# Routing logits placed by hand inside the next tile's output projection, and the normalised rows stored from ScalarE's queue

## The chip, the cores and the metric

The kernel runs on one core of a Trainium2 chip. The metric is device time in microseconds (us) of one execution. Engines are named as in the profile: PE is TensorE, DVE VectorE, ACT ScalarE, POOL GpSimd, SP SyncE; a "queue" is the list of DMAs that one of them issues.

## The reference

Two layers over 512 latent tokens of width 1024, in float32. Each layer adds a token mixer and then a mixture of experts to the stream, each behind an RMSNorm with shift and scale and in front of a gate:

```
for i in range(2):
    h  = modulate(x, norm_mix[i], shift, scale)
    y  = deltanet_mixer(h, ...) if i == 0 else shortconv_mixer(h, ...)    # both end in  ... @ w_out
    x  = x + gate_m * y
    hf = modulate(x, norm_ffn[i], shift_f, scale_f)
    pg = softmax(hf @ router_g[i]);  gi = argmax(pg)                      # one of 4 groups
    le = (hf @ router_e[i])[8 experts of that group];  top 2 of softmax(le)
    x  = x + gate_f * sum over the 2 experts of  weight * (silu(hf @ w1[e]) * (hf @ w3[e])) @ w2[e]
return rmsnorm(x, final_norm)
```

There are 32 experts per layer with a hidden width of 512. What the change touches lies between `x + gate_m * y` and the top 2: the last projection `@ w_out`, the gated sum, the norm, and the 36 logits (4 groups and 32 experts) of each token.

## The kernel before, in words

Tokens are held in four tiles of 128 in the on-chip stream `xs` (128 partitions, 4 tiles, 1024). Projections are computed as 128 by 512 blocks in PSUM: a job is one tile `t` and one half `n` of the 1024 output columns. Numbers are split into a high and a low part, so that a job takes 24 matmuls of 128 x 512: for each of 8 slices `k`, high by high, low by high, high by low.

Weights come as units of 2 MB through rings of buffers, nine units in all. SP issues these loads (`issue`, L214); a load whose buffer is still read waits, and what SP issues behind it waits too. Instructions are put into their order within each engine by a scheduler that models the time; a part of the program inside `manual_schedule` keeps the order in which it is written. Before, that holds for the expert stages only.

**Layer 0, end of the mixer** (`finish`). Eight jobs, first half 0 for all tiles, then half 1. A tile is made ready by `prepare` and `turn` (L1231 transposes, L1233 product on VectorE, L1234 high part on ScalarE, low part on GpSimd; the tiles are named `S`, `yhi`, `ylo`, and `vn`, `Ap` for tile 3). The matmuls are L1258 to L1260, into PSUM banks `pp` and `pj`; VectorE multiplies by the gate and adds the old stream (L1269, L1270). From job 5 on, `logits` of the tile finished one job earlier is written behind each job, and that of tile 3 at the end; the scheduler decides where its parts go.

**Logits of a tile** (`logits`). The norm (L340 to L342); eight transposes of `xs` into two PSUM banks (L351); a copy of each to SBUF, one on VectorE (L357), one on ScalarE (L355); eight matmuls of 128 x 36 with the router weights (L360), which the trace shows as two instructions each; the scaled sum into `L` (L361); the normalised row tile `xn` on ScalarE (L362), and its store to the DRAM scratch `hscr`, issued by SP (L363). The SBUF buffers for this are tiles that the mixer no longer needs (`z`, `kp`, `vp`, `xt`, `qe` in layer 0; `xn`, `whi`, `wlo` in layer 1).

**Routing** (`routing`). It waits for the logits of all tiles, then it is a long chain on VectorE (L1311 on) with a few matmuls (L1380); `ra` and `rb` (L1376, L1378) are written into memory that the logits' tiles have left. At its start SP issues three more weight units and the row of gates (L1286). At its end GpSimd gathers the token rows of the first experts from `hscr` (L1418), TensorE transposes them (L1428), and the expert stage begins (products L1442, L1469; transposes of the gate product L1457).

**Layer 1, end of the mixer** (`mixer1`). The first half of the output projection runs slice by slice for all four tiles into four banks (L1820 to L1822), then the second half tile by tile (L1834 to L1836). `add_out` is the gated sum of one job, a multiply (L1850) and an add (L1851) on VectorE; it is written for both halves of a tile behind the tile's second half, and the logits of the tile before behind that. Then the same routing follows.

The stretch from 548 us to the first experts of layer 0, and that from 1318 us to those of layer 1, are called tails below.

Of the kernel before, what the change touches and what calls it, by code (L numbers as in the profile page):

```python
# [13 lines left out]
AF = mybir.ActivationFunctionType  # L14
OP = mybir.AluOpType
# [4 lines left out]
D = 1024  # L20
# [3 lines left out]
EPS = 1e-6  # L24
# [9 lines left out]
class Net:  # L34
# [310 lines left out]
    def logits(self, l, t, xn, h, banks, lb):  # L345

        nc = self.nc
        r = self.norm(t, xn)
        ps = [self.bank(b) for b in banks]
        for c in range(8):  # L350
            nc.tensor.transpose(ps[c // 4][:, 128 * (c % 4):128 * (c % 4) + 128], self.xs[:, t, 128 * c:128 * c + 128], self.ident)  # L351
        for g in range(2):
            p = ps[g].rearrange("p (k d) -> p k d", k=4)
            if g:
                nc.scalar.activation(h[:, 4 * g:4 * g + 4], p, AF.Copy)  # L355
            else:
                nc.vector.tensor_copy(h[:, 4 * g:4 * g + 4], p)  # L357
        p = self.bank(lb)[:, :36]
        for c in range(8):
            nc.tensor.matmul(p, h[:, c], self.wr[:, l, c], start=(c == 0), stop=(c == 7))  # L360
        nc.vector.scalar_tensor_tensor(self.L[:, t], p, r, self.br[:, l], op0=OP.mult, op1=OP.add)  # L361
        nc.scalar.activation(xn, self.xs[:, t], AF.Copy, scale=r)  # L362
        nc.sync.dma_start(self.hscr[128 * t:128 * t + 128], xn)  # L363
# [823 lines left out]
    def finish(self, fp, wo):  # L1187

        nc, I, pb = self.nc, self.I, self.pb
        gt = fp.tile([128, 1024], F32, name="gt0", bufs=1)  # L1190
# [58 lines left out]
        def logits(t):  # L1249
            z, xt = ld[t]  # L1250
            self.logits(0, t, xt, z, ("pc", "ada"), "pc")
        for i, (t, n) in enumerate(jobs):
            yhi, ylo = ys[t]
            hi, lo = wo[n]
            ps = self.bank(("pp", "pj")[i % 2])
            for k in range(8):
                a, b = yhi[k // 4][:, k % 4], ylo[k // 4][:, k % 4]
                nc.tensor.matmul(ps, a, hi[:, k], start=(k == 0), stop=False)  # L1258
                nc.tensor.matmul(ps, b, hi[:, k], start=False, stop=False)
                nc.tensor.matmul(ps, a, lo[:, k], start=False, stop=(k == 7))  # L1260
            if i == 3:
                self.issue(self.taken - 1, 2)
            for u in ahead.get(i, ()):
                if u != 2:
                    prepare(u)
                ys[u] = turn(u)
            xt = ld[t][1]
            x = self.xs[:, t, 512 * n:512 * n + 512]
            nc.vector.tensor_tensor(x, ps, gt[:, 512 * n:512 * n + 512], op=OP.mult)  # L1269
            nc.vector.tensor_tensor(x, x, xt[:, 512 * n:512 * n + 512], op=OP.add)  # L1270
            if i > 4:
                logits(jobs[i - 1][0])
            if i == 7:
                logits(3)
                self.issue(self.taken, 1)
# [3 lines left out]
    def routing(self, l):  # L1279

        tc, nc, I, rt = self.tc, self.nc, self.I, self.rt
        with ExitStack() as cs:
# [3 lines left out]
            nc.sync.dma_start(self.gate, self.row(l, 2, 1))  # L1286
# [114 lines left out]
            nc.vector.tensor_copy(self.most, most)  # L1401

# [320 lines left out]
    def mixer1(self):  # L1723
        tc, nc, I, cp = self.tc, self.nc, self.I, self.cp
        with ExitStack() as cs:
# [3 lines left out]
            with ExitStack() as ws:  # L1729
# [95 lines left out]
                def logits(t):  # L1825
                    xn, h = (wk.tile([128, 8, 128], F32R, name=n).bitcast(F32) if t > 1 or n == "wlo" else
                             wk.tile([128, 8, 128], F32, name="xn") for n in ("whi", "wlo"))
                    self.logits(1, t, xn.rearrange("p k d -> p (k d)"), h, *(('tr', 'tr'), 'tr'))
                hi, lo = second
                for t in range(4):  # L1830
                    o = slice(128 * t, 128 * t + 128)
# [43 lines left out]
```

## Time and profile before

| | |
|---|---|
| three runs | 1878.93, 1885.66, 1885.20 us; median 1885.2 |
| the profiled execution | 1881.79 us, of which the span of instructions is 1880.0 us |
| granted clock of TensorE, mean over the span | 0.961 of full speed |
| TensorE busy | 1717.0 us, 91% of the span |
| VectorE, ScalarE, GpSimd busy | 43%, 26%, 22% |
| DMA | 307 GB/s of HBM traffic over the span; 425 GB/s in the expert stages |

The busy shares are averages over stages of different kinds. The timelines give the start of an instruction, or of several alike in a row, its duration, and in brackets how long its engine stood idle before it and what ended that. Matmuls overlap: each of 128 x 512 is shown with 0.39 us, and one starts every 0.23 us.

### The profile page before, as it was taken

To read this page: it belongs to the slowest core of one execution; us is meant where nothing else is said; L and a number is where in the kernel's file an instruction comes from. 1 tells how busy PE (TensorE), PEld (TensorE's weight loads), DVE (VectorE), ACT (ScalarE), POOL (GpSimd) and SP (SyncE) were. 2 spreads that over 40 slices of the span, in tenths; PEclk is the share of its full clock that TensorE was granted. 3 is DMA by queue.
4 is the path that set the end of the run, shared out by engine and by line. 5 is a ranking of instruction groups with operands and counts; after the bars stand their busy time and mean duration, and the time that the engine had idled before them with its cause. 6 is when DMAs were issued, how large, how long until landed. Compare 5 with 4: busy or idle time off the path is not lost. (4 is left out here: it accounts for less than half of the span.)

```text
span 1880.0 us, 26579 instructions
## 1 busy us (share of the span) xinstructions
PE 1717.0 (91%) x10245; PEld 988.9 (53%) x10246; DVE 812.6 (43%) x1594; ACT 482.7 (26%) x886; POOL 413.5 (22%) x298
## 2 busy tenths in 40 slices
PE   5999978997987899999999988999789999999996
PEld 4766667776866443434434326688634344444332
DVE  5434877746764232322323328533613233323233
ACT  4465354423213111111111014233211111111112
POOL 1114464725410101111010104343101011111100
PEclk9999999998998899999999999999899999999998
DMA  9579975779927699999998953705679969999992
GB/s 330 191 243 337 312 214 148 172 173 268 249 85 312 264 427 424 427 425 425 425 427 334 401 210 143 281 11 185 258 322 425 426 267 426 425 426 425 426 405 105
DMA packets 154547, 572.33 MB, mean 304 GB/s; under 512 B 55204, under 2 KB 79957, under 8 KB 126210
## 3 DMA queue, kind: packets, MB, share of 16 engines
q1 hardware_dynamic: 149474, 559.45, 77.9%
q0 software_dynamic: 4896, 10.48, 1.5%
q8 instruction: 115, 1.88, 0.4%
q14 instruction: 62, 0.51, 0.1%
HBM read 550.86 MB, written 26.38 MB: 307 GB/s over the span
## 5 line engine op out<-in xcount | busy, mean ns | idle before, releaser
L1442 PE MATMUL pj<-w,hT 128*64 128x512 f32 x2048 | 482.2, 604 | 7.8 <-DMA w<-in_w 2.4
L1507 DVE TENSOR_TENSOR xs<-pj,xs 128x512 f32<-128x512 f32 x264 | 170.5, 686 | 373.4 <-PE pj L1506 369.9
L1442 PEld LDWEIGHTS pj<-w,hT 128*64 128x64 f32 x2048 | 154.0, 138 | 277.1 <-issue 260.7
L1469 PE MATMUL pj<-w,gT 128*64 128x512 f32 x960 | 212.6, 595 | 3.1 <-DVE hT L1434 1.4
L1480 POOL TENSOR_TENSOR ylo<-g,yhi 128x512 fp32r<-128x512 f32 x56 | 70.8, 1264 | 645.5 <-ACT yhi L1479 645.5
L638 POOL TENSOR_TENSOR wlo<-w,whi 128x1024 fp32r<-128x1024 f32 x43 | 106.4, 2478 | 227.7 <-ACT whi L636 226.2
L1469 PEld LDWEIGHTS pj<-w,gT 128*64 128x64 f32 x960 | 77.6, 137 | 117.1 <-issue 109.3
L1475 DVE SCALAR_TENSOR_TENSOR g<-pj,wsl,gate 128x512 f32<-128x512 f32 x64 | 48.1, 751 | 180.3 <-PE pj L1469 164.1
L1505 PE MATMUL pj<-yhi,sel 128*128 128x512 f32 x264 | 117.2, 444 | 5.0 <-PEq L1579 4.3
L1459 ACT ACTIVATE gT<-tr 128x512 f32<-128x512 f32 x32 | 19.1, 597 | 382.5 <-PE tr L1457 382.5
L1505 PEld LDWEIGHTS pj<-yhi,sel 128*128 128x128 f32 x264 | 49.3, 187 | 119.8 <-issue 98.5
L653 PE MATMUL pj<-w,whi 128*128 128x512 f32 x336 | 105.4, 394 | 0.5 <-ACT whi L636 0.5
L1506 PE MATMUL pj<-ylo,sel 128*128 128x512 f32 x264 | 104.1, 394 | 1.4 <-POOL ylo L1480 1.4
L653 PE MATMUL pj<-hhi,wlo 128*128 128x512 f32 x224 | 92.9, 415 | 8.7 <-POOL wlo L638 7.1
L653 PE MATMUL pj<-hhi,whi 128*128 128x512 f32 x224 | 92.5, 413 | 8.3 <-DVE cv L769 5.8
L653 PE MATMUL pj<-hlo,whi 128*128 128x512 f32 x224 | 90.7, 405 | 0.0
L1479 ACT ACTIVATE yhi<-g 128x512 fp32r<-128x512 f32 x62 | 39.0, 630 | 195.4 <-DVE g L1475 195.4
L653 PEld LDWEIGHTS pj<-w,whi 128*128 128x128 f32 x336 | 63.9, 190 | 15.0 <-ACT whi L636 1.0
L636 ACT ACTIVATE whi<-w 128x1024 fp32r<-128x1024 f32 x53 | 55.2, 1052 | 54.2 <-PE pj L653 37.6
L1448 ACT ACTIVATE g<-pj 128x512 f32<-128x512 f32 x32 | 19.1, 597 | 185.8 <-PEq L1572 141.8
L653 PE MATMUL pj<-w,wlo 128*128 128x512 f32 x168 | 66.5, 396 | 0.0
L1432 ACT ACTIVATE hT<-tr,m 128x128 f32<-128x128 f32 x128 | 48.1, 456 | 64.6 <-PE tr L1428 62.9
(606 smaller groups left out, 2701.8 us busy)
## 6 DMA issues: line engine op xcount, KB each, us to landing
w<-in_w SPq DMA_DIRECT2D x188, 2048.0 KB
w<-in_ada_w SPq DMA_DIRECT2D x20, 2048.0 KB
w<-in_w_in_a SPq DMA_DIRECT2D x8, 2048.0 KB
w<-in_w_in_b SPq DMA_DIRECT2D x6, 2048.0 KB
w<-in_ada_w SPq DMA_DIRECT2D x8, 1024.0 KB
w<-in_w SPq DMA_DIRECT2D x8, 1024.0 KB
Y<-R SPq DMA_DIRECT2D x20, 256.0 KB
vp<-vscr SPq DMA_DIRECT2D x18, 256.0 KB
```

Of the source, the lines that this page charges most:

```text
L636: nc.scalar.activation(hi[:, :, :n], w, AF.Copy)
L638: (lo_eng or nc.gpsimd).tensor_tensor(lo[:, :, :n], w, hi[:, :, :n].bitcast(F32), op=OP.subtract)
L653: nc.tensor.matmul(out, n[j][0][:, k], n[j][1][:, k, a:b], start=(i == 0), stop=(i == 23))
L1432: nc.scalar.activation(hT[:, c], q, AF.Identity, bias=self.m8[:, l, 2, c:c + 1], scale=self.m8[:, l, 0, c:c + 1])
L1442: nc.tensor.matmul(ps[64 * x:64 * x + 64], hT[:, k, 64 * x:64 * x + 64], w[x][:, k], start=(k == 0), stop=(k == 7))
L1469: nc.tensor.matmul(py[64 * x:64 * x + 64], gT[:, k, 64 * x:64 * x + 64], w[x][:, k, 512 * n:512 * n + 512], start=(k == 0), stop=(k == 3))
L1475: nc.vector.scalar_tensor_tensor(y, py, wi, self.gate[:, 512 * n:512 * n + 512], op0=OP.mult, op1=OP.mult)
L1479: nc.scalar.activation(o[0][:, c], y, AF.Copy)
L1480: eng.tensor_tensor(o[1][:, c], y, o[0][:, c].bitcast(F32), op=OP.subtract)
L1505: nc.tensor.matmul(ps, s, yhi[:, c], start=True, stop=False)
L1506: nc.tensor.matmul(ps, s, ylo[:, c], start=False, stop=True)
L1507: nc.vector.tensor_tensor(self.xs[:, t, c], ps, self.xs[:, t, c], op=OP.add)
```

## The change

The logits become generators that stop between their steps, and the loops over the jobs step them at chosen slices `k` of the next job, with the order kept as written.

In the first tail, from job 5 on: in slice 2 of a job, the norm, the eight transposes and the copies of the tile finished before; in slice 6, its logits matmuls and what follows them. The last tile (`logits_last`) has the first half of its columns transposed in slice 1 of the last job, since that half of `xs` has been ready for long; the other half, and the logits, come behind the job's sum. The same is done in the second tail for tiles 0 to 3, and all four sums of the first half are written ahead of tile 0's second half. All transposes go through the PSUM tag `tr`, a bank of four transposes at a time; the first copy is ScalarE's, the second VectorE's. The logits use `pc` and `ada` in turn in layer 0, and `pj` in layer 1. `hscr` is stored from ScalarE's queue. The gate row's load stands at the end of `routing`. (`warm` is defined and not called.)

```diff
-    def logits(self, l, t, xn, h, banks, lb):
...
+    def logits(self, l, t, xn, h, lb):
+        r = self.norm(t, xn)
+        for g in range(2):
+            self.turn_half(t, h, g, self.nc.vector if g else self.nc.scalar)
+        yield
+        self.logits_end(l, t, xn, h, lb, r)
+        yield
+    def logits_last(self, l, t, xn, h, lb):
+        nc, s = self.nc, self.ssx[:, :, t:t + 1]
+        nc.scalar.activation(xn[:, :512], self.xs[:, t, :512], AF.Square, accum_out=s[:, 0])
+        nc.vector.tensor_scalar(s[:, 0], s[:, 0], 1.0 / D, EPS, op0=OP.mult, op1=OP.add)
+        self.turn_half(t, h, 0, nc.scalar)
+        yield
+        self.turn_half(t, h, 1, nc.vector)
+        self.logits_end(l, t, xn, h, lb, self.norm(t, xn, self.xs[:, t, 512:]))
+        yield
+    def turn_half(self, t, h, g, eng):
+        p = self.bank("tr")
+        for c in range(4):
+            nc.tensor.transpose(p[:, 128 * c:128 * c + 128], self.xs[:, t, 512 * g + 128 * c:512 * g + 128 * c + 128], self.ident)
...
+    def logits_end(self, l, t, xn, h, lb, r):
         p = self.bank(lb)[:, :36]
         for c in range(8):
             nc.tensor.matmul(p, h[:, c], self.wr[:, l, c], start=(c == 0), stop=(c == 7))
         nc.vector.scalar_tensor_tensor(self.L[:, t], p, r, self.br[:, l], op0=OP.mult, op1=OP.add)
         nc.scalar.activation(xn, self.xs[:, t], AF.Copy, scale=r)
-        nc.sync.dma_start(self.hscr[128 * t:128 * t + 128], xn)
+        nc.scalar.dma_start(self.hscr[128 * t:128 * t + 128], xn)
... finish
+            if i == 5:
+                man.enter_context(self.tc.manual_schedule())
+            if i > 4:
+                side = logits(jobs[i - 1][0])
+            if i == 7:
+                last = logits(t, True)
... in the loop over k
+                if k == 1:
+                    next(last, None)
+                if k in (2, 6):
+                    next(side, None)
...
-            if i > 4:
-                logits(jobs[i - 1][0])
-            if i == 7:
-                logits(3)
-                self.issue(self.taken, 1)
+            next(last, None)
+        self.issue(self.taken, 1)
+        man.close()
... routing
-            nc.sync.dma_start(self.gate, self.row(l, 2, 1))
... at its end
+            nc.sync.dma_start(self.gate, self.row(l, 2, 1))
... mixer1
+                man.enter_context(self.tc.manual_schedule())
                 for t in range(4):
+                    self.add_out(t, 0, po[t], gt, wk)
+                for t in range(4):
+                    side = logits(t - 1) if t else iter(())
+                    last = logits(t, True) if t == 3 else iter(())
... in the loop over k
+                        if k == 1:
+                            next(last, None)
+                        if k in (2, 6):
+                            next(side, None)
-                    self.add_out(t, 0, po[t], gt, wk)
                     self.add_out(t, 1, ps, gt, wk)
-                    if t:
-                        logits(t - 1)
-                logits(3)
+                    next(last, None)
```

How the order of the instructions moves, at the three places that matter most below (a row is a line, an operation, its tiles and shape, and how many alike stand in a row).

TensorE in layer 1, where the first halves of the projection end and tile 0's second half begins (`tr` is the PSUM bank of the transposes). Before, around the transposes of tile 0:

```order
L1834 MATMUL pj<-w 128x512
L1835 MATMUL pj<-w 128x512
L1836 MATMUL pj<-w 128x512
L351 MATMUL tr<-ident,xs 128x128 x8
L1834 MATMUL pj<-w 128x512
```

and in the changed kernel, where L1856 to L1858 are the first half and L1876 on the second:

```order
L1856 MATMUL pj<-whi,w 128x512
L1857 MATMUL pj<-whi,w 128x512
L1858 MATMUL pj<-wlo,w 128x512 x4
L369 MATMUL tr<-ident,xs 128x128 x8
L1876 MATMUL pj<-w 128x512
```

The transposes of tile 0 stood behind triples of second-half matmuls, and now stand directly behind the last first-half matmul, ahead of most of the second half.

VectorE at the same place (`u` is the gated output, `wlo` the transposed rows). Before:

```order
L1758 TENSOR_TENSOR w<-y,w 128x512
L1850 TENSOR_TENSOR u<-pj,gt 128x512 x2
L1851 TENSOR_TENSOR xs<-xs,u 128x512 x2
L1850 TENSOR_TENSOR u<-pj,gt 128x512 x2
L1851 TENSOR_TENSOR xs<-xs,u 128x512 x2
L342 RECIPROCAL ssx<-ssx 128x1
L1850 TENSOR_TENSOR u<-pj,gt 128x512
L1851 TENSOR_TENSOR xs<-xs,u 128x512
L357 COPY wlo<-tr 128x512
```

and in the changed kernel, up to the copy of tile 0's second four transposes:

```order
L1894 TENSOR_TENSOR u<-pj,gt 128x512
L1895 TENSOR_TENSOR xs<-xs,u 128x512
L1894 TENSOR_TENSOR u<-pj,gt 128x512
L1895 TENSOR_TENSOR xs<-xs,u 128x512
L1894 TENSOR_TENSOR u<-pj,gt 128x512
L1895 TENSOR_TENSOR xs<-xs,u 128x512
L1894 TENSOR_TENSOR u<-pj,gt 128x512
L1895 TENSOR_TENSOR xs<-xs,u 128x512
L1894 TENSOR_TENSOR u<-pj,gt 128x512
L1895 TENSOR_TENSOR xs<-xs,u 128x512
L342 RECIPROCAL ssx<-ssx 128x1
L372 COPY wlo<-tr 128x512
```

The ten operations are the first-half sums of tiles 0 to 3 and the second-half sum of tile 0, each multiply now followed by its own add; the last pair is what the second four transposes read.

SP's queue in the first tail (`w` is a weight unit, `grow` the gate row). Before:

```order
L363 DMA hscr<-xt 128x1024
L363 DMA hscr<-qe 128x1024
L214 DMA w<-in_w 128x4096 x2
L363 DMA hscr<-vp 128x1024
L214 DMA w<-in_w 128x4096 x4
L363 DMA hscr<-qe 128x1024
L1286 DMA gate_5845<-grow 128x1024
L214 DMA w<-in_w 128x4096
```

and in the changed kernel:

```order
L214 DMA w<-in_w 128x4096
L1226 DMA qe<-in_x 128x1024
L1225 DMA vp<-zscr 128x1024
L214 DMA w<-in_w 128x4096 x6
L1437 DMA gate_5850<-grow 128x1024
L214 DMA w<-in_w 128x4096
```

The four stores have left this queue (they stand on ScalarE's), the six weight loads stand in one run, and the gate row is at the same place behind them.

## Rows read from the trace of the kernel before

**Rows 1.** Busy time of the engines by stretch: start and end us, length us, busy us of TensorE (PE), its weight loads (PEld), VectorE (DVE), ScalarE (ACT) and GpSimd (POOL) with instructions, the granted clock of TensorE, the busy share of the DMA engines, GB/s. The second row lies within the first expert stage.

```profile
590.00:602.00 12.00, 9.70 (x55) 8.68 (x55) 2.17 (x6) 4.19 (x6) 0.00 (x0) 0.67 1.00 423
...
800.00:920.00 120.00, 116.78 (x519) 48.74 (x516) 36.45 (x64) 16.08 (x33) 15.81 (x14) 1.00 1.01 425
```

**Rows 2.** First expert stage. From the timeline of TensorE (columns: start us, duration us, engine and line, operation with output <- inputs, tile and type, instructions in the row, idle time before it and what ended that) the first transposes of the gate product in two consecutive pairs of experts; last, from the waits of TensorE over 624 to 1070 us (engine, tile and line, what it waited for: us in total, times, longest), the only wait of its products for weights above 0.2 us.

```profile
673.49 0.72 PE L1457 MATMUL tr<-ident,g 128*128 128x128 f32 x4
...
702.25 0.72 PE L1457 MATMUL tr<-ident,g 128*128 128x128 f32 x4 [0.15 <-PEq L1588]
...
PE pj L1442 <- DMA w<-in_w: 2.4, 1, 2.4
```

**Rows 3.** Timeline of TensorE and VectorE at the early half of tile 1's logits; columns as in rows 2.

```profile
548.23 0.60 PE L351 MATMUL pc<-ident,xs 128*128 128x128 f32 x4
...
549.03 0.68 DVE L357 COPY z<-pc 128x512 f32<-128x512 f32 x1
...
549.77 1.08 PE L360 MATMUL pc<-wr,z 128*128 128x36 f32 x8
...
550.23 1.28 DVE L1233 TENSOR_TENSOR kp<-tr,kp 128x512 f32<-128x512 f32 x2
...
551.63 0.50 PE L1258 MATMUL pp<-w,S 128*128 128x512 f32 x1 [0.78 <-ACT S L1234]
```

**Rows 4.** Timelines at the turn of tile 3: a TensorE slot behind its transposes, and the first write of `vn` on ScalarE.

```profile
563.76 0.39 PE L1258 MATMUL pp<-w,S 128*128 128x512 f32 x1
...
564.17 0.63 ACT L1234 ACTIVATE vn<-vp 128x512 fp32r<-128x512 f32 x1 [9.64 <-DVE vp L1233]
```

**Rows 5.** Timeline of TensorE in the last projection of layer 0 and behind it.

```profile
580.44 0.60 PE L351 MATMUL ada<-ident,xs 128*128 128x128 f32 x4
...
581.11 0.39 PE L1259 MATMUL pj<-w,Ap 128*128 128x512 f32 x1
...
587.48 0.39 PE L1260 MATMUL pj<-lo,vn 128*128 128x512 f32 x1
...
589.25 1.98 PE L360 MATMUL pc<-wr,kp 128*128 128x36 f32 x16 [0.44 <-DVE kp L357]
...
591.06 0.63 PE L351 MATMUL ada<-ident,xs 128*128 128x128 f32 x4
```

**Rows 6.** Timeline of VectorE: the first instruction of the routing of layer 0, and the second `rb` of it, with its wait.

```profile
602.14 0.17 DVE L1311 TENSOR_REDUCE gm<-L 128x4 f32<-128x16 f32 x1
...
614.33 0.35 DVE L1378 TENSOR_SCALAR rb<-col,colm,rid 128x128 f32<-128x128 f32 x1 [2.60 <-DMA hscr<-qe]
```

**Rows 7.** First tail: the queue of SP (SPq, when DMAs were issued, and how many), the first gather's issue on GpSimd, and TensorE's first transposes of what it brought.

```profile
587.67 1.88 SPq L214 DMA_DIRECT2D w<-in_w  x4
...
592.80 0.33 SPq L363 DMA_DIRECT2D hscr<-qe  x1
...
619.36 1.21 POOL L1418 DMA_INDIRECT hg<-hscr,gxc  x1 [5.71 <-DVE gs L1367]
...
624.10 1.97 PE L1428 MATMUL tr<-ident,hg 128*128 128x128 f32 x8 [0.71 <-DMA hg<-hscr,gxc]
```

**Rows 8.** DMA issues, from two answers: the gathers within 680 to 760 us, in the expert stage, and the first two gathers, within 615 to 627 us. Columns: tiles, queue, operation and count, median us from issue to landing.

```profile
hg<-hscr,gix POOLq DMA_INDIRECT x3, 11.6
...
hg<-hscr,gxc POOLq DMA_INDIRECT x2, 4.9
```

**Rows 9.** Second tail, timeline of TensorE: a matmul of tile 0's second half, the transposes of tile 0 (24 such matmuls later), the first transposes behind the last projection, and the last logits.

```profile
1319.17 0.39 PE L1834 MATMUL pj<-w 128*128 128x512 f32 x1
...
1324.62 1.03 PE L351 MATMUL tr<-ident,xs 128*128 128x128 f32 x8
...
1335.22 0.60 PE L351 MATMUL tr<-ident,xs 128*128 128x128 f32 x4
...
1342.11 1.98 PE L360 MATMUL tr<-wr,wlo 128*128 128x36 f32 x16 [0.25 <-DVE wlo L357]
```

**Rows 10.** Second tail, timeline of VectorE: the first sums of the output (`add_out`), the last ones, and the first instruction of the routing of layer 1.

```profile
1318.46 1.29 DVE L1850 TENSOR_TENSOR u<-pj,gt 128x512 f32<-128x512 f32 x2 [18.45 <-PE pj L1822]
...
1335.42 0.69 DVE L1850 TENSOR_TENSOR u<-pj,gt 128x512 f32<-128x512 f32 x1 [2.02 <-PE pj L1836]
...
1336.14 0.69 DVE L1851 TENSOR_TENSOR xs<-xs,u 128x512 f32<-128x512 f32 x1
...
1344.41 0.17 DVE L1311 TENSOR_REDUCE gm<-L 128x4 f32<-128x16 f32 x1
```

**Rows 11.** Second tail: the last store and the gate row on SP's queue, the first gather's issue, and TensorE's first transposes of it.

```profile
1340.34 0.33 SPq L363 DMA_DIRECT2D hscr<-whi  x1
...
1356.41 0.33 SPq L1286 DMA_DIRECT2D gate<-grow  x1
...
1358.44 1.10 POOL L1418 DMA_INDIRECT hg<-hscr,gxc  x1 [2.18 <-DVE tid L1386]
...
1367.38 1.95 PE L1428 MATMUL tr<-ident,hg 128*128 128x128 f32 x8 [3.58 <-DMA hg<-hscr,gxc]
```

**Rows 12.** Busy time and granted clock of TensorE around a short idle stretch ahead of the last projection of layer 0: start and end us, length, PE busy (instructions), granted clock, DMA share, GB/s.

```profile
528.00:533.50 5.50, 0.51 (x1) 0.93 0.07 28
...
533.50:539.00 5.50, 5.42 (x13) 0.50 0.00 0
...
540.00:542.00 2.00, 2.00 (x12) 1.00 0.00 0
```

More of the change, by code (lines that the diff above doesn't have):

```diff
@@ L343, in norm @@
         return s[:, 2]
-    def logits(self, l, t, xn, h, banks, lb):
-        nc = self.nc
[L348 to L357, printed above, removed]
+    def logits(self, l, t, xn, h, lb):
[15 more added lines that the diff above has]
+    def turn_half(self, t, h, g, eng):
+        nc = self.nc
+        p = self.bank("tr")
+        for c in range(4):
+            nc.tensor.transpose(p[:, 128 * c:128 * c + 128], self.xs[:, t, 512 * g + 128 * c:512 * g + 128 * c + 128], self.ident)
+        p = p.rearrange("p (k d) -> p k d", k=4)
+        if eng is nc.vector:
+            eng.tensor_copy(h[:, 4 * g:4 * g + 4], p)
+        else:
+            eng.activation(h[:, 4 * g:4 * g + 4], p, AF.Copy)
+    def logits_end(self, l, t, xn, h, lb, r):
+        nc = self.nc
         p = self.bank(lb)[:, :36]
@@ L362, in logits, with warm @@
         nc.scalar.activation(xn, self.xs[:, t], AF.Copy, scale=r)
-        nc.sync.dma_start(self.hscr[128 * t:128 * t + 128], xn)
+        nc.scalar.dma_start(self.hscr[128 * t:128 * t + 128], xn)
+    def warm(self, n):
+        p = self.bank("pj")
+        for _ in range(n):
+            self.nc.tensor.matmul(p, self.ident, self.xs[:, 0, :512], start=True, stop=True)
     def router(self, l, row):
@@ L1247, in finish, with logits @@
         ahead = {0: (2,), 1: (0,), 2: (3,)}
-        def logits(t):
+        def logits(t, last=False):
             z, xt = ld[t]
-            self.logits(0, t, xt, z, ("pc", "ada"), "pc")
+            return (self.logits_last if last else self.logits)(0, t, xt, z, ("pc", "ada")[t % 2])
+        man = ExitStack()
         for i, (t, n) in enumerate(jobs):
+            side = last = iter(())
+            if i == 5:
[4 more added lines that the diff above has]
+                last = logits(t, True)
             yhi, ylo = ys[t]
@@ L1824, in mixer1, with logits @@
                 self.issue(self.taken, 9)
-                def logits(t):
+                def logits(t, last=False):
                     xn, h = (wk.tile([128, 8, 128], F32R, name=n).bitcast(F32) if t > 1 or n == "wlo" else
                              wk.tile([128, 8, 128], F32, name="xn") for n in ("whi", "wlo"))
-                    self.logits(1, t, xn.rearrange("p k d -> p (k d)"), h, *(('tr', 'tr'), 'tr'))
+                    return (self.logits_last if last else self.logits)(1, t, xn.rearrange("p k d -> p (k d)"), h, "pj")
                 hi, lo = second
+                man = ExitStack()
+                man.enter_context(self.tc.manual_schedule())
                 for t in range(4):
+                    self.add_out(t, 0, po[t], gt, wk)
+                for t in range(4):
+                    side = logits(t - 1) if t else iter(())
+                    last = logits(t, True) if t == 3 else iter(())
                     o = slice(128 * t, 128 * t + 128)
@@ L1836, in mixer1 @@
                         nc.tensor.matmul(ps, yhi[:, k, o], lo[:, k], start=False, stop=(k == 7))
-                    self.add_out(t, 0, po[t], gt, wk)
+                        if k == 1:
+                            next(last, None)
+                        if k in (2, 6):
+                            next(side, None)
                     self.add_out(t, 1, ps, gt, wk)
-                    if t:
-                        logits(t - 1)
-                logits(3)
+                    next(last, None)
+                man.close()
                 ring[2][-4:] = [-1 if i == 9999 else i for i in ring[2][-4:]]
```

## The prediction

> **What bounds the kernel now.** I read the profile from the outside in. The busy times by stretch come first: in the expert stages TensorE is busy 97% of the time while the DMA engines run at 425 GB/s [rows 1]. One pair of experts takes 28.76 us there (702.25 - 673.49), its 12.6 MB take 29.6 us at 425 GB/s, and in the whole first expert stage a weight was late only once, by 2.4 us [rows 2]. So TensorE sets the pace, a later or earlier start of an expert stage is passed on to the end, and time can be won only ahead of those stages. The change works in the two stretches there, where the last projection of a mixer ends and the routing begins. Call them the first tail (548 to 624 us) and the second tail (1318 to 1367 us). In each I read four views: the timelines of TensorE and VectorE, the queue of SP, and the waits of the routing and of its first gather on the DMA.
>
> **First tail, TensorE and VectorE.** The old code has an early half of tile 1's logits at 548 us. Its copy out of PSUM stands on VectorE ahead of the product `kp` that leads to the next projection matmul, which is 0.78 us late at 551.63 [rows 3]. Without them `kp` can start at about 549.1 instead of 550.23: -1.1 us (at most the 0.60 + 1.08 us of the removed TensorE work, at least nothing).
>
> Then the order loses a cover. Job (0,1), 24 matmuls, stood behind the eight transposes of tile 3 and hid their way through VectorE and ScalarE. Now tile 3's first matmul stands there, and its `vn` is written by 564.80 while TensorE is free at 563.76 [rows 4]: +1.0 us.
>
> Into the projections go 20 more transposes and 20 more logits matmuls than stood among them. Four transposes cost 0.44 us in a dense stream (580.44 to 581.11 less one matmul of 0.23), eight logits matmuls 1.81 us (589.25 to 591.06) [rows 5]: 5 x 0.44 + 20/8 x 1.81 = +6.7 us. The last projection, which ends at 587.87 [rows 5], then ends at 587.87 - 1.1 + 1.0 + 6.7 = 594.5.
>
> What follows it is shorter. Before, two and a half tiles of logits stood there, 14.3 us up to the first routing instruction at 602.14 [rows 6]. Now four transposes and the logits of one tile are left: multiply and add on VectorE, 1.6 us from the last matmul's slot (1335.22 to 1336.83 in [rows 9, 10]), transposes 0.60 [rows 5], copy 0.68 [rows 3], and the last four logits matmuls with the evacuation, 1.4 us (1342.11 to 1344.41 less half of 1.81, [rows 9, 10]). That is 4.3 us, so the routing starts at 598.8: **-3.3 us**.
>
> **First tail, the stores.** In the routing, VectorE stands 2.60 us at the second `rb`, whose memory is freed by the last store of `hscr` [rows 6]. That store was issued at 592.80 behind four weight loads of 587.67 on SP's queue [rows 7]. On ScalarE's queue it no longer stands behind them, but shares the engines with them: the loads wait for the end of the last projection, so they start at 594.5, and the store follows the last add by 3.5 us as in the second tail (1336.83 to 1340.34, [rows 10, 11]), at about 599.6. The same 512 KB as a gather on a third queue take 4.9 us on idle engines and 11.6 us among loads [rows 8]. `rb` wants the memory at 598.8 + 9.6 = 608.4, so the wait is between 0 and 2.8 us; I take 1.0: **-1.6 us**, with nothing to -2.6 as ends.
>
> **First tail, the gather.** This is what is late next. Before, it was issued at 619.36 when the loads had drained, and its transposes ran at 624.10, 4.7 us later [rows 7]. Now it is issued at 614.5, but four loads, the gate row, one more load and a store, 11.5 MB or 27.1 us at 425 GB/s [rows 1], have run only since 594.5, to 621.6. The nearest row is the second tail's gather, which met loads and took 8.9 us (1358.44 to 1367.38, [rows 11]): 623.4 instead of 624.10. **First tail in all: -0.7 us**, between -5.8 (no wait, gather as if alone) and +2.4 (both as if under load).
>
> **Second tail, TensorE.** The new order writes all four first-half sums (`add_out` of n = 0) ahead of tile 0's second half, and TensorE's eight transposes of tile 0 stand right behind the last first-half matmul. Before, 57 matmuls of second halves were left at 1319.17 and eight triples of them stood ahead of the transposes; the DVE work was hidden by them [rows 9, 10]. Now 63 are left, so the point is reached 6 x 0.227 = 1.4 us earlier, at 1317.8. There the first four transposes wait for two VectorE operations and the other four for ten. Ten cost 5 x 0.72 (a dependent add behind its multiply, 1335.42 to 1336.14) + 4 x 0.60 (two at 1318.46 take 1.29, one takes 0.69) + 0.69 - 0.07 = 6.6 us from 0.5 us before the point [rows 10], less 0.44 for the transposes in between: TensorE stands **5.7 us**. Everything behind it queues: 63 x 0.227 + 7 x 0.44 + 3 x 1.81 = 22.8 us, last projection at 1346.3, routing 4.3 us later at 1350.6 instead of 1344.41: +6.2 us. Less can't be had: before, TensorE ran through here without a gap worth the name.
>
> The clock is the next term. At 528 to 533 us TensorE had almost nothing to do for about as long; the granted clock fell from 1.00 to 0.50, that is from 2.4 to 1.2 GHz, and was back at 1.00 by 540, so that matmuls from 533.6 on ran at half speed for some 5.5 us [rows 12]. The same here costs half of about 5 us: +2.4, between 0 (it does not fall) and +3.
>
> Then the gather. Loads, gate row, load and store (9.4 MB, 22.2 us) begin with the last projection's end, 1348.7, and drain at 1370.9; the gather is issued 14.0 us behind the routing's start, at 1367.0, and finds 3.9 us of loads. Before, it found about as much (gate row and load issued from 1356.41, 2.6 MB, 6.2 us; gather at 1358.44, [rows 11]). So again 8.7 us or so: 1375.7 instead of 1367.38. **Second tail: +8.3 us**, between +2.0 (no fall of the clock, gather alone 4.9) and +11.2.
>
> **What costs nothing.** The issue of eight stores on ScalarE's queue lies beside its idle time in both tails. The gate row is emitted later, but stands at the same place of SP's queue, and is needed only at the first down product, some 25 us behind the transposes. The nine units in the ring have landed by 624 and 1371, before the first experts free a slot about 12 us later, so no load is late in the expert stages for it.
>
> **The sum.** -0.7 + 8.3 = +7.6 us. The profiled execution took 1881.8 us (span 1880.0), 3.4 below the median of the three runs, 1885.2, and the four together have a mean of 1882.9. I set the sum on that mean: 1890.5, rounded to **1890 us**.
>
> **A rule that speaks against the stores' move.** The Trainium skill, "Trainium Kernel Development and Optimization", Key Constraints, says that DMAs from the queues of SP, ACT and POOL run on the same 16 engines and that issuing from several engines only saves issue time. Its page "DMA: Bandwidth & Descriptors" (Queues, rings and completion order) says that each DMA engine takes turns between the queues that have work, by which the store would be served among the loads. The rows lean to the second: POOL's gather took 11.6 us among loads, SP's store 21 us behind them [rows 6 to 8].
>
> **Rivals.** (1) *The store still lands behind the loads.* Then `rb` waits until 594.5 + 21.0 (four loads and a store) = 615.5, 7.1 us instead of 2.6; the gather is issued at 620.6 on nearly idle engines and lands at about 626: first tail +2, in all 1893. Against it stands POOL's gather. Chance 0.10. (2) *The gather of the first tail is not held up* and the clock does not fall in the second: -5.8 and +6.2, in all 1883, no change; where the second gather, too, comes as if alone, 1879. For it speaks that the loads of both tails are nearly drained when the gather comes, against it the 8.9 us of [rows 11]. Chance 0.22. (3) *Slower:* in the second tail the clock falls and stays at 0.50 up to the routing, because batches of transposes and 36-column matmuls now stand between short runs of projection matmuls. The price is the 22.8 us once more, less the 2.4 already counted: +20, in all 1911; from about 7 us at half speed on it is over 0.5%. For it: in the first tail the clock fell while such small matmuls ran (0.67 in the stretch from 590 to 602, [rows 1]). Against it: dense matmuls brought it back within 6 us at 533 [rows 12]. Chance 0.13. The forecast, with both ends of its terms, keeps 0.55.
>
> **How the numbers follow.** About 0.5%, 9.4 us, is what a measurement of this kernel can tell from no change. The forecast's own range is 1882 to 1896; a tenth or more of the chance lies over 1894.6. With rival (2) down to 1879 and part of rival (3) the range is 1879 to 1899. Slower takes rival (3), 0.13, and the upper part of the forecast and of (1), 0.12; faster needs the low end of (2) and a run like the lowest of 1878.9, 0.05.
>
> **What would show it.** Right: TensorE idle between the eight transposes of tile 0 in the second tail, released by VectorE's `xs`, 4 to 6 us, and the granted clock at 0.50 behind it; routing of the first tail some 3 us earlier, its `rb` wait gone or small, and the wait of the first transposes on the gather larger. Wrong: no such idle time, or a first gather that comes within 5 us, or a store on ScalarE's queue that lands later than 12 us after its issue.

## The result, and the profile after

The changed kernel takes 1892.5 us (median of 6 runs, 1888.22 to 1899.78), the kernel before 1883.1 (median of 6 runs): a ratio of 1.0054, with a 95% interval of 1.0040 to 1.0069. That is 9.4 us slower by the medians and 10.2 us by the ratio. The forecast was 1890.

The profiled execution of the changed kernel is the slowest of the six (1899.78 us, span 1897.5). 6.1 us of what it is longer than the trace of the kernel before lie ahead of the change: the last matmul of the second job, up to which TensorE's order is the same, starts at 554.11 and not at 547.99. The runs show no effect of the change in this: in the traces of the nine experiments that matmul starts between 546.48 and 551.16, with the new first tail and with the old one. So both tails are read from a common point of their own.

First tail, the common point in the kernel before (TensorE):

```profile
547.99 0.39 PE L1260 MATMUL pj<-w,yhi 128*128 128x512 f32 x1
```

and in the changed kernel the timelines of TensorE and VectorE (`gm` is the routing's first instruction, L1292 to L1294 the projection, L369 the transposes and L380 the logits, L1464 the transposes of gathered rows):

```profile
554.11 0.39 PE L1294 MATMUL pj<-w,yhi 128*128 128x512 f32 x1
...
556.55 0.50 PE L1292 MATMUL pp<-w,S 128*128 128x512 f32 x1 [1.17 <-ACT S L1260]
...
600.31 0.39 PE L1294 MATMUL pj<-lo,vn 128*128 128x512 f32 x1
602.30 0.63 PE L369 MATMUL tr<-ident,xs 128*128 128x128 f32 x4 [1.60 <-DVE xs L1308]
602.77 2.94 PE L380 MATMUL ada<-wr,vp 128*128 128x36 f32 x16
...
606.03 0.17 DVE L1346 TENSOR_REDUCE gm<-L 128x4 f32<-128x16 f32 x1
...
615.87 0.36 DVE L1413 TENSOR_SCALAR rb<-col,colm,rid 128x128 f32<-128x128 f32 x1 [0.25 <-DMA hscr<-qe]
...
632.61 1.97 PE L1464 MATMUL tr<-ident,hg 128*128 128x128 f32 x8 [6.94 <-DMA hg<-hscr,gxc]
```

The queues there:

```profile
600.54 1.94 SPq L214 DMA_DIRECT2D w<-in_w  x4
602.53 0.53 SPq L1437 DMA_DIRECT2D gate<-grow  x1
603.10 0.46 SPq L214 DMA_DIRECT2D w<-in_w  x1
...
605.01 0.33 ACTq L383 DMA_DIRECT2D hscr<-qe  x1
...
620.34 1.23 POOL L1454 DMA_INDIRECT hg<-hscr,gxc  x1 [2.55 <-DVE tid L1421]
```

Counted from that last matmul of the second job, in us:

| | before | forecast | after |
|---|---|---|---|
| next projection matmul [rows 3] | 3.64 | 2.5 | 2.44 |
| end of the last projection [rows 5] | 39.9 | 46.5 | 46.6 |
| routing begins [rows 6] | 54.2 | 50.8 | 51.9 |
| `rb` waits for the store [rows 6] | 2.60 | 1.0 | 0.25 |
| first gather issued [rows 7] | 71.4 | 66.5 | 66.2 |
| its rows transposed [rows 7] | 76.1 | 75.4 | 78.5 |

So the start of the routing came 2.2 us earlier and the issue of the gather 5.1 us, and the gather then took 12.3 us where it had taken 4.7.

Second tail, TensorE (L1858 the last first-half matmuls, L1876 to L1878 the second half):

```profile
1326.26 1.07 PE L1858 MATMUL pj<-wlo,w 128*128 128x512 f32 x4
1328.16 0.65 PE L369 MATMUL tr<-ident,xs 128*128 128x128 f32 x4 [0.83 <-DVE xs L1895]
1333.47 1.12 PE L369 MATMUL tr<-ident,xs 128*128 128x128 f32 x4 [4.66 <-DVE xs L1895]
...
1357.71 0.40 PE L1878 MATMUL pj<-w 128*128 128x512 f32 x1
1359.71 0.63 PE L369 MATMUL tr<-ident,xs 128*128 128x128 f32 x4 [1.60 <-DVE xs L1895]
1360.17 2.53 PE L380 MATMUL pj<-wr,wlo 128*128 128x36 f32 x16
...
1374.86 3.35 PE L1415 MATMUL pj<-rb,ra 128*128 128x128 f32 x14 [1.45 <-POOL ra L1411]
...
1384.86 1.94 PE L1464 MATMUL tr<-ident,hg 128*128 128x128 f32 x8 [1.62 <-DMA hg<-hscr,gxc]
```

and TensorE's busy time and granted clock in three stretches (start and end us, length, PE busy, clock, DMA share, GB/s):

```profile
1330.00:1334.00 4.00, 0.53 (x3) 0.60 0.01 4
1334.00:1338.00 4.00, 4.00 (x13) 0.55 0.18 73
1338.00:1342.00 4.00, 4.00 (x27) 1.00 0.14 58
```

SP's queue, the stores' queue, VectorE and GpSimd there:

```profile
1357.90 1.28 SPq L214 DMA_DIRECT2D w<-in_w  x3
1359.29 0.62 SPq L1437 DMA_DIRECT2D gate<-grow  x1
1359.96 0.52 SPq L214 DMA_DIRECT2D w<-in_w  x1
...
1362.35 0.33 ACTq L383 DMA_DIRECT2D hscr<-whi  x1
1363.03 0.17 DVE L1346 TENSOR_REDUCE gm<-L 128x4 f32<-128x16 f32 x1
...
1373.46 0.60 POOL L1323 IOTA tok<- 128x512 f32 x1 [50.38 <-PE pj L1415]
...
1378.88 1.10 POOL L1454 DMA_INDIRECT hg<-hscr,gxc  x1 [2.29 <-DVE tid L1421]
```

The transposes of tile 0 wait 0.83 and 4.66 us for VectorE's `xs`. In the second stop and behind it the granted clock is 0.60 and 0.55, between its two levels of 1.2 and 2.4 GHz, and the matmuls of 1334 to 1337 start every 0.43 us in place of 0.23. At the end of the projection there is a third stop, 1.60 us.

The next table counts from the end of the last first-half matmul (1327.17). Before, six second-half matmuls more stood ahead of that point; their 1.4 us are taken off, 1319.17 - 1.36 = 1317.81:

| | before | forecast | after |
|---|---|---|---|
| end of the last projection [rows 9] | 17.4 | 30.9 | 30.8 |
| routing begins [rows 10] | 26.6 | 35.2 | 35.9 |
| first gather issued [rows 11] | 40.6 | 49.2 | 51.7 |
| its rows transposed [rows 11] | 49.6 | 57.9 | 57.7 |

That is +8.1 us, where +8.3 was forecast. The two tails give +2.4 and +8.1; of the 17.5 us between the two spans the other 6.1 lie ahead of the change and 0.9 between the tails.

### The profile page after: what moved, and what is told of

The parts are those of the page before. It is cut to its first block, busy times and chain, and to the rows that moved or that the text cites. A ratio compares the mean times of both kernels' runs of the same rounds, so it can differ in the third digit from the quotient of the medians.

```text
span 1897.5 us, 26581 instructions
## 1 busy us (share of the span) xinstructions
PE 1717.5 (91%) x10245; PEld 987.1 (52%) x10246; DVE 817.2 (43%) x1596; ACT 482.2 (25%) x890; POOL 414.8 (22%) x298
## 5 line engine op out<-in xcount | busy, mean ns | idle before, releaser
L679 PE MATMUL pj<-w,wlo 128*128 128x512 f32 x168 | 66.2, 394 | 0.0
```

Source lines behind the costliest of these rows:

```text
L679: nc.tensor.matmul(out, n[j][0][:, k], n[j][1][:, k, a:b], start=(i == 0), stop=(i == 23))
```

## The experiments

Each was timed in turns with the kernel before; the ratio is to that, with its 95% interval, and us are the ratio's difference from 1 times 1882; by this count the changed kernel has +10.2. A difference between two kernels of less than some 4 us is not clear of the intervals. Stretches of time within a kernel are read from its one profiled execution: with the same order of instructions, the first tail up to the transposed rows took 77.6 to 78.9 us in six traces.

### One sum ahead instead of four

```diff
-                for t in range(4):
-                    self.add_out(t, 0, po[t], gt, wk)
+                self.add_out(0, 0, po[0], gt, wk)
...
                     self.add_out(t, 1, ps, gt, wk)
+                    if t < 3:
+                        self.add_out(t + 1, 0, po[t + 1], gt, wk)
```

> The changed kernel, but in the second tail the first-half sums of tiles 1 to 3 are not written ahead of all second halves: each stands behind the second-half sum of the tile before it. Theory (TensorE's stop in the second tail costs the time): the second four transposes of tile 0 then wait for four VectorE operations and not for ten; TensorE's idle time there falls from 5.5 us (0.83 + 4.66 in the changed kernel) to about 1.5, the granted clock does not fall to 0.50 behind it (2.4 us more), and the kernel takes about 6 us less than the changed one: 1886, a ratio of 1.002 to the kernel before. Rival (the gather among the weight loads sets the tail, TensorE's stop is covered by it): the routing starts earlier, the wait for the gather grows by as much, 1892, ratio 1.005.

1.0038 (1.0024 to 1.0052), +7.2 us: 3 us less than the changed kernel, within the intervals. The stops of TensorE, from its timeline:

```profile
1321.75 0.66 PE L369 MATMUL tr<-ident,xs 128*128 128x128 f32 x4 [0.83 <-DVE xs L1896]
1323.08 0.66 PE L369 MATMUL tr<-ident,xs 128*128 128x128 f32 x4 [0.67 <-DVE xs L1896]
...
1340.10 0.63 PE L369 MATMUL tr<-ident,xs 128*128 128x128 f32 x4 [1.54 <-DVE xs L1896]
...
1349.11 0.63 PE L369 MATMUL tr<-ident,xs 128*128 128x128 f32 x4 [1.60 <-DVE xs L1896]
```

The stop of 4.66 us is 0.67, and the granted clock from 1320 to 1332 is 1.00. The theory of the stop holds: in the trace the routing begins 4.7 us earlier behind the end of the first halves than in the changed kernel, and the rows are transposed 4.1 us earlier. Of the 6 us expected a part is missing, because tile 3's first half now waits for its sum, 1.54 us, a place that the expectation had left out. The four stops make 4.64 us; from the end of the first halves to the routing it takes 4.56 us more than the next kernel, which has none of them.

### The second tail as before, the stores on ScalarE's queue

```diff
-                man.enter_context(self.tc.manual_schedule())
... (the loop of the second tail, logits and add_out in it, as before the change)
+                    self.add_out(t, 0, po[t], gt, wk)
+                    self.add_out(t, 1, ps, gt, wk)
+                    if t:
+                        logits(t - 1)
+                logits(3)
```

> The changed kernel with the second tail as it was before (order by the scheduler, sums behind the second half of each tile), except that the stores stay on ScalarE's queue. Theory: what is left is the first tail, whose trace shows +2.4 us to the first transposes of gathered rows: 1885.5, ratio 1.001. If the gather among loads had been a matter of that one profiled run, -0.7: 1882.5, ratio 0.9996. Rival (the loss sits in the first tail): 1892, ratio 1.005.

0.9986 (0.9973 to 0.9999), -2.6 us. So the order of the second tail costs 12.8 us (10.2 + 2.6), more than the whole change, and the rest of the change wins a little. The first tail takes 78.4 us up to the transposes, as in the changed kernel; but the second, from the end of the first halves, takes 44.9 us and not 48.2 as before, which the theory did not have. Its gather takes 5.6 us where it took 8.9; the next run shows why.

### The stores alone

```diff
-        nc.sync.dma_start(self.hscr[128 * t:128 * t + 128], xn)
+        nc.scalar.dma_start(self.hscr[128 * t:128 * t + 128], xn)
```

in the kernel before.

> The kernel before with one edit, the stores of the normalised rows issued by ScalarE. Theory: the last store of the first tail no longer stands behind four loads, the 2.60 us wait of the second rb for it goes or nearly goes, the gather is issued 2 to 2.6 us earlier and meets a little more of the loads; -1.5 us, between 0 and -2.6: 1881.5, ratio 0.9992. Second tail unchanged. Rival (the store shares the engines with the loads and lands as late): the wait stays at 2 to 3 us, 1883, ratio 1.000.

0.9971 (0.9955 to 0.9987), -5.5 us, more than expected. In the first tail the wait of `rb` is gone and the trace shows -2.0 us, as the theory had it; -3.3 us came in the second tail, which the theory had called unchanged. There the kernel before had this wait on SP's queue (engine and line, what it waited for: us in total, times, longest):

```profile
SPq L1286 <- DMA hscr<-whi: 15.7, 1, 15.7
```

and with the stores moved the queue and the gather are:

```profile
1333.44 1.28 SPq L214 DMA_DIRECT2D w<-in_w  x3
1349.17 0.33 SPq L1286 DMA_DIRECT2D gate<-grow  x1
...
1356.72 1.10 POOL L1418 DMA_INDIRECT hg<-hscr,gxc  x1 [2.18 <-DVE tid L1386]
...
1362.30 1.82 PE L1428 MATMUL tr<-ident,hg 128*128 128x128 f32 x8 [0.22 <-DMA hg<-hscr,gxc]
```

The gate row waits for the last store to land. With the store behind three loads that was at 1356.41, and the gate row and the last load, behind it on the queue, then fell on the gather of 1358.44 [rows 11], which took 8.9 us. Now they go out 7.5 us ahead of the gather, and it takes 5.6.

### The stores back on SP's queue

The changed kernel with L383 as `nc.sync.dma_start`.

> The changed kernel with its stores issued by SP as before; the last store of the first tail then stands behind three of the loads that wait for the last projection. Theory: three loads and a store, 6.8 MB, take 16 us from the end of the last projection, so rb waits 2 to 3 us instead of 0.25 and the gather is issued later by as much, but it lands when the loads have drained anyway: the first transposes come 0 to 2 us later; in the second tail the store lands about when the gather is issued, 0 to 2 us. 1892 to 1895, ratio 1.005 to 1.007. Rival (the store's queue decides the first tail): each microsecond of the wait is passed on and the gather takes as long as before, 1897, ratio 1.0075.

1.0079 (1.0061 to 1.0096), +14.9 us. That is the rival's time, but not by its way. In the first tail `rb` waits 3.54 us, the gather is issued 3.5 us later and takes 7.8 us and not 12.3: the transposes come 77.5 us behind the common point, no later than with the store on ScalarE's queue. The end of the loads decides there, not the issue of the gather. In the second tail the store behind the loads costs 4.2 us, which the theory had put at 0 to 2:

```profile
1352.12 0.33 SPq L383 DMA_DIRECT2D hscr<-whi  x1
1352.54 0.38 SPq L1437 DMA_DIRECT2D gate<-grow  x1
...
1368.79 0.56 POOL L1323 IOTA tok<- 128x512 f32 x1 [55.71 <-DMA hscr<-whi]
...
1374.02 1.10 POOL L1454 DMA_INDIRECT hg<-hscr,gxc  x1 [2.34 <-DVE tid L1421]
...
1379.04 1.14 PE L1464 MATMUL tr<-ident,hg 128*128 128x128 f32 x8
```

GpSimd's iota waits for the store, and the gather, issued 5.1 us later behind the end of the first halves than in the changed kernel, takes 5.0 us. The gate row, right behind the store on the same queue, does not wait for it to land here.

### The last load held until the gather has landed

The kernel with the old second tail, and in the first tail:

```diff
-            hT = turn(gather(col(self.gxc, 0)))
+            hg0 = gather(col(self.gxc, 0))
+            if l == 0:
+                nc.sync.dma_start(self.dr.tile([1, 1024], F32, name="held"), hg0[0:1])
+                nc.sync.dma_start(self.gate, self.row(l, 2, 1))
+            hT = turn(hg0)
             self.issue(self.taken, 1)
... at the end of routing
-            nc.sync.dma_start(self.gate, self.row(l, 2, 1))
+            if l:
+                nc.sync.dma_start(self.gate, self.row(l, 2, 1))
```

> The kernel of the run with the old second tail, and in the first tail SP now copies one row of the first gathered tile to DRAM before it issues the gate row and the last weight load, so that these two start only when the first gather has landed. Theory (the early routing of the first tail is given back because its gather runs among the loads): the four loads drain at about the time at which the gather is issued, the gather takes about 5 us instead of 11.95, and the first transposes of gathered rows come 7 us earlier, 71.5 us behind the last matmul of the first half-tile job instead of 78.43; no weight comes later in the expert stage, since the late one there has 2.4 us in every run so far: 1873, ratio 0.995 to the kernel before. Rival (the gather is slow for itself, from the state of its queue or memory): 1879.5 as without the hold, ratio 0.9986. Rival (the held load is missed later): the wait for weights in the expert stage grows by what is won, 1879.5.

0.9964 (0.9950 to 0.9979), -6.8 us, 4 us less than without the hold. The queue, the gather's issue and its transposes:

```profile
592.91 2.06 SPq L214 DMA_DIRECT2D w<-in_w  x4
619.73 0.26 SPq L1619 DMA_DIRECT2D held<-hg  x1
620.03 0.34 SPq L1620 DMA_DIRECT2D gate<-grow  x1
...
612.92 1.23 POOL L1475 DMA_INDIRECT hg<-hscr,gxc  x1 [2.55 <-DVE tid L1441]
...
619.76 1.97 PE L1485 MATMUL tr<-ident,hg 128*128 128x128 f32 x8 [2.43 <-DMA hg<-hscr,gxc]
```

The gather takes 6.8 us, more than the 5 expected, and the transposes come 73.3 us behind the common point, 5.2 earlier than without the hold, where 7 were expected. The wait for weights in the expert stage stays 2.5 us, once. Both rivals fall. With the stores alone this is the fastest kernel here; the two are not told apart.

### The gate row behind the last load

The kernel before with the gate row's DMA moved from the start of `routing` to behind `self.issue(self.taken, 1)` in `moe`; stores on SP.

> The kernel before with one edit: the gate row is issued behind the last weight load and not ahead of it; stores stay on SP. Theory (in the second tail the gate row waits 15.7 us for the last store to land and holds the last weight load behind it, so that the load falls on the gather; the stores' move cures that): the last load goes out with the other three, the gather takes 5.6 us instead of 8.9, -3.3 us in the second tail; in the first tail the last store is now behind five loads, so rb waits up to 4.9 us longer and the gather finds idle engines: 0 to +5. 1880 to 1885, with the second tail's gather as the evidence. Rival (the gather of the second tail is helped by the store's earlier landing itself): the gather stays at 8.9 us.

1.0021 (1.0011 to 1.0031), +4.0 us. The second gather takes 4.9 us in place of 8.9, where 5.6 was expected, so its rival falls; but now the last store stands behind four loads, and the gather is issued 4.0 us later, which was not expected. In the first tail `rb` waits 8.37 us, and 4.9 us are lost, the upper end. The gate row alone is no cure: what stands behind the loads, store or load, is waited for.

### GpSimd's iota behind the rows of `ra`

The changed kernel with the `iota` of L1323 moved to the end of `routing`.

> The changed kernel with one instruction moved: GpSimd's iota for the token numbers stands behind the four ra that it writes in the routing, and not ahead of them. In the changed kernel that iota ran at 1373.46 us, 11.1 us behind the issue of tile 3's store at 1362.35, the four ra behind it, and TensorE stood 1.45 us for ra. Theory (the iota writes memory that tile 3's store still reads, and the store takes 11 us among the loads): without it ahead, ra runs when its rows are there, and the second tail's gather is issued 14.0 us behind the start of the routing, as before the change, and not 15.85; the gather itself takes up to as much longer, since the loads drain no earlier. Total 0 to -1.8 us: 1891.5, ratio 1.0045. Rival (ra itself waits for the store, or GpSimd for something else): 15.85 stays, 1892.5, ratio 1.005.

1.0059 (1.0041 to 1.0077), +11.1 us, the same time as the changed kernel.

```profile
1369.67 1.09 POOL L1454 DMA_INDIRECT hg<-hscr,gxc  x1 [1.65 <-DVE tid L1420]
...
1377.42 1.76 PE L1464 MATMUL tr<-ident,hg 128*128 128x128 f32 x8 [2.67 <-DMA hg<-hscr,gxc]
```

The gather is issued 14.1 us behind the start of the routing, not 15.85, and takes 7.75 us, not 5.98; the transposes come at the same time behind the end of the first halves, within 0.01 us. The theory's wait was there, and cost nothing, because the loads drain no earlier.

### Work in the stop, and the same work elsewhere

```diff
             self.turn_half(t, h, g, self.nc.vector if g else self.nc.scalar)
+            if l == 1 and t == 0 and g == 0:
+                self.warm(4)
```

and, in a second kernel, `t == 1`.

> The changed kernel with four matmuls of 128 x 512 in float32 that compute nothing of use between the first and the second four transposes of tile 0 in the second tail, where TensorE stood idle 4.66 us. Theory (the clock falls because of that stop, and the matmuls behind it run at half speed for some 4 us): the idle time stays where it was but is filled, the granted clock is 1.00 from 1334 to 1338 us in place of 0.55, and the last projection ends about 2.2 us earlier, as the routing does: 1890.3, ratio 1.004. Rival (the extra matmuls take longer than the idle time and delay the transposes, or the clock falls all the same): 1892.5 or more, ratio 1.005 or more.

1.0020 (1.0008 to 1.0032), +3.8 us, 6.4 less than the changed kernel. The extra matmuls, the transposes behind them, and TensorE's clock behind the stop:

```profile
1318.83 3.60 PE L391 MATMUL pj<-xs,ident 128*128 128x512 f32 x8
1323.65 0.66 PE L371 MATMUL tr<-ident,xs 128*128 128x128 f32 x4 [1.21 <-DVE xs L1897]
...
1324.00:1328.00 4.00, 4.00 (x26) 1.00 0.14 55
```

The clock does not fall, and the last projection ends 1.9 us earlier, where 2.2 was expected. But the clock falls sooner behind the last projection (the last logits take 3.47 us and not 2.53), so that the routing begins 0.6 us earlier and the rows are transposed 1.5 us earlier. The other 5.5 us lie at the end of the program, in the last pair of experts.

> The changed kernel with the same four extra matmuls as in the run before it, but between the transposes of tile 1 in the second tail, where TensorE has no idle time to fill. Of the 7 us that the run before won, its trace shows 1.5 in the second tail and 5.5 in the last pair of experts (59.0 us from its first transposes to the end, 64.5 in the changed kernel), where a stop of TensorE of 1.76 us that nothing explains is missing. Theory (the place of TensorE's code, 16 instructions further on, decides that stop): the end takes 59.0 us again, the second tail is longer by the four matmuls, 3.6 us, and the stop of 4.66 us and the fall of the clock behind tile 0's transposes are as in the changed kernel: 1890.6, ratio 1.005. Rival (the end depends on what went before, the clock or the state of the tail): the end takes 64.5 us, 1896, ratio 1.008.

1.0054 (1.0037 to 1.0072), +10.2 us, as the changed kernel; the second tail is 3.8 us longer, with the stop of 4.65 us and the clock at 0.50 again. TensorE's last products in the changed kernel,

```profile
1868.64 1.04 PE L1523 MATMUL pj<-w,gT 128*64 128x512 f32 x2 [2.35 <-ACT dummy L323]
1871.44 9.79 PE L1523 MATMUL pj<-w,gT 128*64 128x512 f32 x30 [1.76 <-issue]
```

with the work in the stop,

```profile
1857.69 7.09 PE L1525 MATMUL pj<-w,gT 128*64 128x512 f32 x32 [2.31 <-ACT dummy L323]
```

and with it one tile later:

```profile
1862.14 8.78 PE L1525 MATMUL pj<-w,gT 128*64 128x512 f32 x32 [2.46 <-ACT dummy L323]
```

The stop of 1.76 us behind the first two products is gone in both, so it goes with the extra matmuls, at both places where they stood. That the place of the code decides it, as the theory has it, is not shown, but fits the other traces: the stop stands behind the fourth product in the three kernels with the old order in both tails, behind the third in the two with the new first tail alone, and behind the second in the four with both new tails. The end takes 60.8 us in the second kernel, not 59.0, since the clock still falls there (0.57 from 1863 to 1867). Why it does in one and not in the other is open.

## Why the prediction was right

**The second tail's stop** was sized right: 0.83 + 4.66 us against 5.7. The forecast's 22.8 us of dense work then leave 2.5 us for the lower clock, against 2.4, so that the last projection ended 0.1 us off. The experiments show both causes: without the long stop the clock stays at 1.00, and with work in the stop it stays too, which won 1.9 us up to the end of the projection. The scheduler's order had no gap there to fill; the kernel with the old second tail shows that the second tail's order by hand costs 12.8 us. In the traces that kernel's second tail is 11.4 us shorter, 9.3 of them before the routing begins: the stops of 0.83, 4.66 and 1.60 us, and the clock. The end of the program, 64.5 us against 62.7 for the last pair of experts, makes 1.8 us more.

**The first tail's work** was right to 0.1 us up to the last projection. The short end behind it was mis-sized: 5.3 us, not 4.3 (5.1 in the second tail). All eight logits matmuls stand behind the last transposes, not four, and ran partly at the lower clock (granted 0.79 from 602 to 605 us; 2.94 us for what took 1.87 at 598.06).

**The gathers were mis-sized both ways.** The first took 12.3 us where 8.9 were taken; the wrong step is "the nearest row is the second tail's gather". Five loads, the gate row, a store and the first two gathers, which GpSimd issues one behind the other, all issued from 600.5 on, are 12.6 MB, 29.6 us at the 425 GB/s of [rows 1], which makes 630.1; the first gather's rows were transposed from 632.6 on. The forecast's 11.5 MB had left the gathers' own bytes out. The same estimate holds in the second tail: four loads, the gate row, a store and two gathers from 1357.9 on are 10.5 MB and 24.7 us, which makes 1382.6, and the rows were transposed from 1384.9 on. A gather issued among the loads landed when all of this had drained. The upper end of the range, +2.4 us, is what came, but that is luck: the two ends that it names, a wait of 2.8 us and a gather of 11.6, add up to +3.8.

The second gather took 6.0 us where 8.7 were taken. In the kernel before, that gather met the gate row and a load behind it that waited for the last store; the wait stood as 15.7 us in the waits of SP's queue, a view that the prediction had not read. The sentence that the gate row "stands at the same place of SP's queue" was true and missed this. In the changed kernel the gate row goes out at 1359.29, before the last store is even issued, so it is not the stores' move that frees it there: with the stores back on SP's queue the gate row does not wait either, and the gather takes 5.0 us. In the five kernels with the old second tail the gate row waited 14 to 21 us for the last store, in the six with the new one it did not. There GpSimd's iota waited for it, named in the traces of four of them: the new order moved the wait to another engine.

**What was late next** was missed once: that iota, 1.8 us. It cost nothing.

The errors in the second tail are +0.7 us (the routing), +1.8 (the iota) and -2.7 (the gather). The last two are one thing in part: where the end of the loads decides, a gather issued 1.8 us later is 1.8 us shorter, as the run with the iota moved shows. That the rest cancels to -0.2 is luck. In the first tail the error of +3.1 us stays, and the forecast had the wrong sign. So the sum of 7.6 us, against 10.5 in the two tails of the traces and 9.4 to 10.2 in the times, is better than its parts. By kernels it splits otherwise than forecast: the stores -5.5 us where -1.6 was forecast, the first tail's order +2.9 (within the intervals; 4.3 in the traces), the second's +12.8.

**The rivals.** The gather of the first tail was held up, and the clock fell (rival 2 falls; its second half, a gather nearly as if alone, came in the second tail). The clock did not stay at 0.50 up to the routing (rival 3 falls: it was 1.00 again from 1338). The store on ScalarE's queue does not land behind the loads (rival 1 falls): `rb` saw it 10.9 us behind its issue, against 21.5 before [rows 6, 7]. By the Trainium skill, "DMA: Bandwidth & Descriptors", Queues, rings and completion order, the queues with work are served in turn; the trace agrees. The Trainium skill, "Trainium Kernel Development and Optimization", Key Constraints, says that issuing from several engines only saves issue time. That does not hold where the queue is held by loads ahead: here the stores' move alone saved 5.5 us, and the issue of one store takes 0.33.

## What to carry to other kernels

In a stretch where TensorE had no idle time, the order by hand could only add stops: ask of each instruction put between dense work how many operations of the other engine it waits for. Read the waits of a DMA queue, not only of the engines: what stands behind a store that stands behind loads waits with it, and no engine shows that until it falls on the next transfer. A gather that was issued earlier into running loads landed when they had drained; holding the last load until it had landed won 4 us.

## What the runs showed of the hardware

TensorE stopped 1.5 to 1.9 us in the last products of nine of the eleven kernels, with nothing in the profile that it waited for, and the granted clock fell behind it (over the next 4 us 0.50 in six of the kernels and 0.62 to 0.66 in three). Eight more matmul instructions earlier in the program took the stop away at both places where they were tried. The last pair of experts took 62.4 to 64.5 us in the nine kernels with the stop and 59.0 and 60.8 us in the two without it. So two kernels that differ in TensorE's code can differ by 2 to 5 us at the end, as much as an edit of the first tail was worth, and what causes the stop is open.
